# Transposed probabilities copied ahead of the next weight split, and their low part used last in the value product

## The chip, the core and the metric

The kernel runs on one core of one Trainium2 chip. The time is the device time of one launch in microseconds; three timed runs of the kernel before gave 2951.14 us in the median (2946.77 to 2953.13). The changed kernel is timed against it in the same way.

Five engines work side by side, each through its own queue in the order in which the program was written: TensorE (PE, with its weight loads listed apart as PEld), VectorE (DVE), ScalarE (ACT), GpSimd (POOL) and SyncE (SP), which here only issues DMAs. They wait for each other by semaphores.

## What is computed

Two layers of a decoder trunk over 256 tokens of width 2048, all in float32:

```
u = RMSNorm(x);  z = u @ W_in          # parts: cq, ckv+rope key, xb, yb, gate a, gate r
A = causal attention, 16 heads         # low-rank q and kv, a rotary key of 64
R = gelu(yb) * RG-LRU(conv4(xb))
x = x + (sigmoid(ga) * A + sigmoid(gr) * R) @ W_out
x = x + relu(RMSNorm(x) @ W_up)^2 @ W_down
x = x + sigmoid(RMSNorm(x) @ W_pg) * (p[layer] @ W_pe)
```

In the attention, each head has its scores, a softmax `pr`, and the product with the values:

```
pr = softmax(where(causal, sc * scale, -inf))
out = einsum('bhqk,bkhd->bqhd', pr, v)
```

## The kernel before

**Products in three parts.** A float32 operand is split in a high part (rounded to the format that TensorE reads fast) and a low part (the rest). A product is then three matmuls: high weight by high activation, high by low, low by high (`mm3`, L216 to L218).

**Weights in halves.** All weights come in 1004 halves of 128x1024 float32 (512 KB), in the order of use. `half()` hands out the next one. Before it does, it lays out the split of the half that is used two steps later (`split_half`: `hi` on ACT at L122, `lo` on DVE at L126), and then lets the planner (`work`) lay out as many waiting jobs as fit on ACT and DVE within the estimated time of the coming half. There are three buffers each for `hi` and `lo`, so `hi` of half h+2 can only start when TensorE is done with half h-1. A usual half is 24 matmuls.

**Jobs.** `later(key, steps, rank)` puts a job (a row of ACT and DVE steps) in a list by rank; `need(key)` lays out whatever of a job is missing at once (`force`), since TensorE's next instruction depends on it. The planner goes by estimated costs in `E`; what it lays out first stands first in the engine's queue for good.

**The mixer.** Each layer goes through 8 groups of two heads. A group computes xb, yb, k, v, q, the rotary part of q (qr), the recurrence gates (lru), the gates gr and ga, as products from halves; and between the halves of a gate, by hooks, its attention: `scores(0)`, `scores(1)` (tile `s`) in gr, then in ga `turned(0)` after its first half, `values(0)` and `turned(1)` after its second, `values(1)` after its third. In group 0 the late three stand in the xb product of group 1 instead.

`turned(t)` transposes the probabilities of head t on TensorE in three pieces (tile `pt`, L959 to L961) and puts off the job ("pt", t) at rank -2: the copy of the transposed tile to the high part `pt_hi` (ACT, L964), and the rest to `pt_lo` (DVE, L967). `values(t)` needs that job and multiplies (tile `o`): for each of two blocks of keys (256 and 128 query columns) `mm3` with the high and low value tile as weights and `pt_hi`, `pt_lo` as moving data; so the second of its six matmuls reads `pt_lo`. There is one buffer each for `pt_hi`, `pt_lo`, `pt` and `o`.

In group 0, `rot_kr` puts off the rotation of the rotary key (job ("rot", k)), four small ACT copies `sw_k`, three DVE steps, and its split `krk`.

The last group's merged result (`bufB` in layer 0, `bufA` in layer 1, tiles 14 and 15) is read by the product `out` that follows the mixer; its first two pairs of halves go in crossed order, so tiles 14 and 15 are first read at the end of its third half.

Of the kernel before, what the change touches and what calls it, by code (L numbers as in the profile page):

```python
# [18 lines left out]
P = 128  # L19
S = 256  # L20
# [56 lines left out]
def trunk_kernel(ctx: ExitStack, tc: tile.TileContext, xT, pT, pos, par, gfin, invf, wu, out):  # L77
# [13 lines left out]
    V, A, T, G = nc.vector, nc.scalar, nc.tensor, nc.gpsimd  # L91

    def f(ap):
        return ap.bitcast(F32)
# [12 lines left out]
    def load_to(h):  # L107
        while nxt["dma"] <= min(h, n_halves - 1):
            load(nxt["dma"])
            nxt["dma"] += 1  # L110
# [3 lines left out]
    E = {"P": 0.0, "V": 0.0, "A": 0.0, "G": 0.0}  # L114
# [18 lines left out]
    jobs, done = [], {}  # L133
# [3 lines left out]
    class Job:  # L137
# [14 lines left out]
        def step(self, start):  # L152
            eng, cost, fn = self.steps.popleft()
            fn()
            E[eng] = self.ready = start + cost
            if not self.steps:
                jobs.remove(self)
                for k in self.keys:
                    done[k] = self.ready

# [9 lines left out]
    def later(key, *steps, deps=(), rank=1, also=()):  # L170

        job = Job((key, *also), rank, deps, steps)
        at = len(jobs)
        while at and jobs[at - 1].rank > rank:
            at -= 1
        jobs.insert(at, job)

    def need(key):

        if key not in done:  # L180
            next(j for j in jobs if key in j.keys).force()
        E["P"] = max(E["P"], done[key] + LATENCY)
# [19 lines left out]
    def half():  # L202
        h = nxt["used"]
        nxt["used"] += 1
        while nxt["half"] <= min(h + min(LA, max(h - 1, 0)), n_halves - 1):
            split_half(nxt["half"])
            nxt["half"] += 1
        load_to(h + PD)
        work(E["P"] + WINDOW + 0.9, E["P"] + WINDOW)
        hi, lo, at = halves.pop(h)  # L210
        E["P"] = max(E["P"], at)
        return hi, lo

    def mm3(o, wh, wl, ah, al, start, stop, shared=False):

        T.matmul(o, lhsT=wh, rhs=ah, start=start, stop=False, skip_group_check=shared)  # L216
        T.matmul(o, lhsT=wh, rhs=al, start=False, stop=False, skip_group_check=shared)  # L217
        T.matmul(o, lhsT=wl, rhs=ah, start=False, stop=stop, skip_group_check=shared)  # L218
        E["P"] += 0.328
# [371 lines left out]
    def split_steps(d, name, src, tag, cols=512):  # L591


        def high():
            d["src"] = src()
            for w in "hl":
                d[w] = att.tile([P, cols], F32R, name=f"{name}{w}", tag=f"{tag}{w}")
            A.activation(d["h"], d["src"], AF.Copy)

        def low():  # L600
            V.tensor_tensor(out=d["l"], in0=d["src"], in1=f(d["h"]), op=ALU.subtract)

        return ("A", 0.5 if cols > S else 0.3, high), ("V", 0.6 if cols > S else 0.35, low)
# [100 lines left out]
    def group(l, g, u, mg, norm, cn, kr, first, rot_kr):  # L704

        nm = f"{l}_{g}"
        h0 = 2 * g
        t_ = {}
# [93 lines left out]
            rows(ps_k[:, t * S:(t + 1) * S], wt, lambda k: slice(k * 256 + t * P, k * 256 + (t + 1) * P), 1)  # L802
        d_k = t_["k"] = {}
        later(("k", nm), *split_steps(d_k, f"k{nm}", lambda: ps_k, "k"), rank=0)
        hi, lo = half()
        ps_v = mm_bank(f"v_{nm}", ("v", nm))
        for j in range(2):
            o = ps_v[:, j * S:(j + 1) * S]
# [14 lines left out]
            rows(ps_q[:, t * S:(t + 1) * S], wt, lambda k: slice(k * 256 + t * P, k * 256 + (t + 1) * P), 0)  # L823
        d_q = t_["q"] = {}
        later(("q", nm), *split_steps(d_q, f"q{nm}", lambda: ps_q, "q"), rank=0)
        if rot_kr is not None:
            rot_kr()
        wt = half()
        ps_p = bank("r", f"qr_{nm}", ("qr", nm))
        rows(ps_p[:, 0:S], wt, lambda k: slice(k * P, (k + 1) * P), 0)  # L830
# [27 lines left out]
        for t in range(2):  # L858
            ps_l = bank("s", f"lru{t}_{nm}", ("lru", t, nm))
            sl = slice(t * S, (t + 1) * S)  # L860
            for w in range(2):
                c = slice(512 + (2 * w + t) * P, 512 + (2 * w + t + 1) * P)
# [92 lines left out]
        def turned(t):  # L955
            need(("p", t, nm))
            e = t_["p", t]
            pt = bank("t", f"pt{t}_{nm}", ("pt", t, nm))
            T.transpose(pt[:, 256:384], e[:, 256:384], ident)  # L959
            T.transpose(pt[:, 384:512], e[:, 0:128], ident)  # L960
            T.transpose(pt[:, 128:256], e[:, 128:256], ident)  # L961

            def high():
                A.activation(PT[0][:, P:512], pt[:, P:512], AF.Copy)  # L964

            def low():
                V.tensor_tensor(out=PT[1][:, P:512], in0=pt[:, P:512], in1=f(PT[0][:, P:512]), op=ALU.subtract)  # L967

            later(("pt", t, nm), ("A", 0.4, high), ("V", 0.5, low), rank=-2)

        def values(t):
            need(("pt", t, nm))
            need(("v", nm))
            o = bank("o", f"o{t}_{nm}", ("o", t, nm))
            h, lo = PT
            for j, c in ((0, slice(S, 512)), (1, slice(P, S))):
                cc = slice(j * S + t * P, j * S + (t + 1) * P)
                mm3(o[:, j * P:S], t_["v"]["h"][:, cc], t_["v"]["l"][:, cc], h[:, c], lo[:, c], j == 0, j == 1)

            def evac():  # L980
                if t == 0:
                    t_["oT"] = att.tile([P, 512], F32, tag="oT", name=f"oT_{nm}")
                A.activation(t_["oT"][:, t * S:(t + 1) * S], o[:, 0:S], AF.Copy)

            later(("o", t, nm), ("A", 0.27, evac), rank=-1)
# [381 lines left out]
```

## Time and profile before

| what | value |
|---|---|
| median of three runs | 2951.14 us (2946.77 to 2953.13) |
| the profiled execution | 2949.3 us, of it 2947.5 us span from first to last instruction |
| TensorE busy | 2907.9 us, 24800 matmuls |
| VectorE, ScalarE busy | 1864.3 us, 1538.9 us |
| granted TensorE clock | 0.998 of full speed over the span |
| DMA | 535 MB, 182 GB/s in the mean |

TensorE is the engine that the time follows; the other two are busy for 63% and 52% of the span. Matmuls are pipelined: a matmul of 256 columns is shown as 0.28 us long, but the next starts 0.11 to 0.12 us after it. So the idle time that the profile shows in front of a matmul is shorter than what the wait costs: the cost is read from the starts.

### The profile page before, as it was taken

Reading aid. Unit: us, or ns where it says so; the run is one execution under the profiler, and the core shown is the slowest. Engines: PE = TensorE matmul, PEld = TensorE weight load, DVE = VectorE, ACT = ScalarE, POOL = GpSimd, SP = SyncE. Lnnn points to the kernel's source line nnn. Section 1 sums busy time; section 2 is a strip of 40 time slices with the busy share of each in tenths; the row PEclk is TensorE's granted clock in tenths of the full one; section 3 lists DMA queues with packets and bytes.
Section 4 is the critical chain, followed back from the end, with each engine's and each line's share of the span. In section 5 each row is a group of like instructions: output and inputs, shape, how many; then the busy total and the mean of one; then the engine's idle time right before and its main releaser. Section 6 shows DMA issues by size and latency. Waiting matters only on the chain.

```text
span 2947.5 us, 58412 instructions
## 1 busy us (share of the span) xinstructions
PE 2907.9 (99%) x24800; PEld 2896.9 (98%) x24800; DVE 1864.3 (63%) x2420; ACT 1538.9 (52%) x2050; POOL 8.9 (0%) x17
## 2 busy tenths in 40 slices
PE   8999999999999999999999999999999999999998
PEld 8999999999999999999999999999999999999998
DVE  7877777765555454556758777776654555555565
ACT  5666666644344343444546666666543444434445
POOL 0000000000000000000000000000000000000000
PEclk9999999999999999999999999999999999999999
DMA  7555455555555555555555555555555555555553
GB/s 238 168 173 178 165 170 175 172 186 186 186 187 186 186 187 187 191 186 190 190 185 171 173 166 166 174 176 177 189 187 187 186 187 187 188 188 190 186 186 129
DMA packets 146998, 535.23 MB, mean 182 GB/s; under 512 B 16560, under 2 KB 16816, under 8 KB 146736
## 3 DMA queue, kind: packets, MB, share of 16 engines
q1 hardware_dynamic: 146736, 531.50, 54.9%
q8 instruction: 194, 3.18, 0.4%
q14 instruction: 68, 0.56, 0.0%
HBM read 529.33 MB, written 2.10 MB: 180 GB/s over the span
## 4 chain that ended last, share of the span: by engine, by line
PE 93%; DVE 3%; ACT 3%; issue 1%; DMA 0%; ACTq 0%; SPq 0%; POOLq 0%
PE down L218 8%; PE up L218 8%; PE down L217 8%; PE down L216 8%; PE up L216 8%; PE up L217 8%; PE yb L217 2%; PE gr L216 2%; PE yb L218 2%; PE yb L216 2%; PE out L217 2%; PE gr L218 2%; PE out L218 2%; PE gr L217 2%; PE out L216 2%; PE pg L217 2%
## 5 line engine op out<-in xcount | busy, mean ns | idle before, releaser
L126 DVE TENSOR_TENSOR lo<-raw,hi 128x1024 fp32r<-128x1024 f32 x1004 | 1229.8, 1225 | 878.5 <-ACT hi L122 876.3
L122 ACT ACTIVATE hi<-raw 128x1024 fp32r<-128x1024 f32 x1004 | 1066.0, 1062 | 1376.3 <-PE down L217 411.5
L216 PE MATMUL up<-bufA,hi 128*128 128x256 f32 x1024 | 287.9, 281 | 0.0
L216 PE MATMUL down<-bufB,hi 128*128 128x256 f32 x1024 | 287.7, 281 | 0.0
L217 PE MATMUL down<-bufB,hi 128*128 128x256 f32 x1024 | 287.7, 281 | 0.0
L218 PE MATMUL down<-bufB,lo 128*128 128x256 f32 x1024 | 287.7, 281 | 0.0
L216 PE MATMUL down<-bufA,hi 128*128 128x256 f32 x1024 | 287.7, 281 | 0.0
L217 PE MATMUL down<-bufA,hi 128*128 128x256 f32 x1024 | 287.7, 281 | 0.0
L218 PE MATMUL down<-bufA,lo 128*128 128x256 f32 x1024 | 287.7, 281 | 0.0
L216 PE MATMUL up<-bufB,hi 128*128 128x256 f32 x1024 | 287.7, 281 | 0.0
L217 PE MATMUL up<-bufA,hi 128*128 128x256 f32 x1024 | 287.6, 281 | 0.0
L218 PE MATMUL up<-bufA,lo 128*128 128x256 f32 x1024 | 287.6, 281 | 0.0
L218 PE MATMUL up<-bufB,lo 128*128 128x256 f32 x1024 | 287.5, 281 | 0.0
L217 PE MATMUL up<-bufB,hi 128*128 128x256 f32 x1024 | 287.5, 281 | 0.0
L217 PEld LDWEIGHTS down<-bufB,hi 128*128 128x128 f32 x1024 | 196.6, 192 | 0.0
L217 PEld LDWEIGHTS down<-bufA,hi 128*128 128x128 f32 x1024 | 196.6, 192 | 0.0
L217 PEld LDWEIGHTS up<-bufA,hi 128*128 128x128 f32 x1024 | 196.4, 192 | 0.0
L217 PEld LDWEIGHTS up<-bufB,hi 128*128 128x128 f32 x1024 | 196.4, 192 | 0.0
L216 PEld LDWEIGHTS up<-bufA,hi 128*128 128x128 f32 x1024 | 192.3, 188 | 0.0
L218 PEld LDWEIGHTS up<-bufB,lo 128*128 128x128 f32 x1024 | 192.2, 188 | 0.0
L218 PEld LDWEIGHTS up<-bufA,lo 128*128 128x128 f32 x1024 | 192.2, 188 | 0.0
L218 PEld LDWEIGHTS down<-bufB,lo 128*128 128x128 f32 x1024 | 192.2, 188 | 0.0
(551 smaller groups left out, 7857.8 us busy)
## 6 DMA issues: line engine op xcount, KB each, us to landing
raw<-wu SPq DMA_DIRECT2D x1004, 512.0 KB, 3.4
y<-rows SPq DMA_DIRECT2D x4, 512.0 KB, 4.0
x<-xT SPq DMA_DIRECT2D x3, 512.0 KB, 8.2
x<-xT SPq DMA_DIRECT2D x2, 256.0 KB, 4.3
praw<-pT SPq DMA_DIRECT2D x2, 256.0 KB, 4.6
parT<-par SPq DMA_DIRECT2D x1, 184.0 KB, 2.5
rope_w<-pos SPq DMA_DIRECT2D x1, 128.0 KB, 4.1
gf<-gfin SPq DMA_DIRECT2D x1, 8.0 KB, 8.1
```

What stands on the lines that cost most here:

```text
L122: A.activation(hi, src, AF.Copy)
L126: V.tensor_tensor(out=lo, in0=src, in1=f(hi), op=ALU.subtract)
L216: T.matmul(o, lhsT=wh, rhs=ah, start=start, stop=False, skip_group_check=shared)
L217: T.matmul(o, lhsT=wh, rhs=al, start=False, stop=False, skip_group_check=shared)
L218: T.matmul(o, lhsT=wl, rhs=ah, start=False, stop=stop, skip_group_check=shared)
```

## The change

Three things.

1. `turned(t)` no longer puts its copies off. A new helper `at_once` makes the job and lays out its steps right there, so `pt_hi` and `pt_lo` stand in the queues of ACT and DVE ahead of the split that the next `half()` lays out.
2. `values(t)` orders its six matmuls so that the four with `pt_hi` come first and the two with `pt_lo` last; the same six products are summed. The planner's estimate for them is 0.6 instead of 0.656.
3. In group 0, `rot_kr` is called right after k, three halves earlier than before.

```diff
+    def at_once(key, *steps):
+
+        Job((key,), 0, (), steps).force()
@@ turned
-            later(("pt", t, nm), ("A", 0.4, high), ("V", 0.5, low), rank=-2)
+            at_once(("pt", t, nm), ("A", 0.4, high), ("V", 0.5, low))
@@ values
-            for j, c in ((0, slice(S, 512)), (1, slice(P, S))):
-                cc = slice(j * S + t * P, j * S + (t + 1) * P)
-                mm3(o[:, j * P:S], t_["v"]["h"][:, cc], t_["v"]["l"][:, cc], h[:, c], lo[:, c], j == 0, j == 1)
+            vh, vl = (t_["v"][w] for w in "hl")
+            ops = [(v, h, j) for j in range(2) for v in (vh, vl)] + [(vh, lo, j) for j in range(2)]
+            for n, (v, q, j) in enumerate(ops):
+                c = slice(P, S) if j else slice(S, 512)
+                T.matmul(
+                    o[:, j * P:S], lhsT=v[:, j * S + t * P:j * S + (t + 1) * P], rhs=q[:, c], start=n == 0, stop=n == 5,
+                    skip_group_check=True,
+                )
+            E["P"] += 0.6
@@ group
         later(("k", nm), *split_steps(d_k, f"k{nm}", lambda: ps_k, "k"), rank=0)
+        if rot_kr is not None:
+            rot_kr()
...
         later(("q", nm), *split_steps(d_q, f"q{nm}", lambda: ps_q, "q"), rank=0)
-        if rot_kr is not None:
-            rot_kr()
```

What this makes of the queues, at the places of the prediction. First ScalarE's queue in group 6 of layer 0, from the first transposes on (`hi157` and `hi158` are the high parts of two coming weight halves, `zz` and `gr` belong to the recurrence and its gate). Before:

```order
L891 ACTIVATE zz_0_6_6056<-zz_0_6_6056 128x512
L122 ACTIVATE hi157_6157<-raw157_5890 128x1024
L964 ACTIVATE pt_hi_125<-pt0_0_6_6153 128x384
L777 ACT_TABLE_LOAD
L777 ACTIVATE gr_0_6_6126<-gr_0_6_6126 128x512
L122 ACTIVATE hi158_6201<-raw158_5928 128x1024
L964 ACTIVATE pt_hi_125<-pt1_0_6_6197 128x384
```

and the same place on ScalarE now:

```order
L896 ACTIVATE zz_0_6_6056<-zz_0_6_6056 128x512
L969 ACTIVATE pt_hi_125<-pt0_0_6_6153 128x384
L122 ACTIVATE hi157_6159<-raw157_5890 128x1024
L782 ACT_TABLE_LOAD
L782 ACTIVATE gr_0_6_6126<-gr_0_6_6126 128x512
L969 ACTIVATE pt_hi_125<-pt1_0_6_6200 128x384
L122 ACTIVATE hi158_6206<-raw158_5928 128x1024
```

Each of the two `pt_hi` has changed places with the `hi` ahead of it. VectorE's queue at the same place in group 6 (`lo157`, `lo158` are the low parts of those halves, `ee`, `thx` and `hh` belong to the recurrence, L901 is its scan). Before:

```order
L774 TENSOR_TENSOR gr_0_6_6126<-gr_0_6_5923,R_mix0_668 128x512
L126 TENSOR_TENSOR lo157_6158<-raw157_5890,hi157_6157 128x1024
L967 TENSOR_TENSOR pt_lo_126<-pt0_0_6_6153,pt_hi_125 128x384
L894 TENSOR_SCALAR ee_0_6_5935<-ee_0_6_5935 128x512
L895 MEMSET ee_0_6_5935 128x2
L896 SCALAR_TENSOR_TENSOR thx_0_6_5934<-thx_0_6_5934,xc_0_6_5650 128x512
L899 TENSOR_TENSOR thx_0_6_5934<-thx_0_6_5934,zz_0_6_6056 128x512
L901 SCALAR_TENSOR_TENSOR hh_0_6_6208<-ee_0_6_5935,thx_0_6_5934 128x512
L126 TENSOR_TENSOR lo158_6202<-raw158_5928,hi158_6201 128x1024
L967 TENSOR_TENSOR pt_lo_126<-pt1_0_6_6197,pt_hi_125 128x384
```

and VectorE now:

```order
L779 TENSOR_TENSOR gr_0_6_6126<-gr_0_6_5923,R_mix0_668 128x512
L972 TENSOR_TENSOR pt_lo_126<-pt0_0_6_6153,pt_hi_125 128x384
L899 TENSOR_SCALAR ee_0_6_5935<-ee_0_6_5935 128x512
L900 MEMSET ee_0_6_5935 128x2
L901 SCALAR_TENSOR_TENSOR thx_0_6_5934<-thx_0_6_5934,xc_0_6_5650 128x512
L126 TENSOR_TENSOR lo157_6160<-raw157_5890,hi157_6159 128x1024
L972 TENSOR_TENSOR pt_lo_126<-pt1_0_6_6200,pt_hi_125 128x384
L126 TENSOR_TENSOR lo158_6207<-raw158_5928,hi158_6206 128x1024
L904 TENSOR_TENSOR thx_0_6_5934<-thx_0_6_5934,zz_0_6_6056 128x512
L906 SCALAR_TENSOR_TENSOR hh_0_6_6215<-ee_0_6_5935,thx_0_6_5934 128x512
```

The first `pt_lo` now stands ahead of `lo157`, the second ahead of `lo158` and of the scan; the scan is the one that has moved back. Third, VectorE at the end of the last group of layer 0, where the merged tiles 14 and 15 of `bufB` are written, before:

```order
L126 TENSOR_TENSOR lo180_7056<-raw180_6779,hi180_7055 128x1024
L1011 SCALAR_TENSOR_TENSOR bufB_90<-ga_0_7_6972,bufB_90 128x256
L1002 SCALAR_TENSOR_TENSOR ga_0_7_6972<-ga_0_7_6972,oT_0_7_6986 128x256
L1005 SCALAR_TENSOR_TENSOR ga_0_7_6972<-hh_0_7_6978,ga_0_7_6972 128x256
L126 TENSOR_TENSOR lo181_7091<-raw181_6827,hi181_7090 128x1024
L1011 SCALAR_TENSOR_TENSOR bufB_90<-ga_0_7_6972,bufB_90 128x256
L126 TENSOR_TENSOR lo182_7124<-raw182_6879,hi182_7123 128x1024
```

and now:

```order
L1018 SCALAR_TENSOR_TENSOR ga_0_7_6980<-hh_0_7_6985,ga_0_7_6980 128x256
L126 TENSOR_TENSOR lo181_7089<-raw181_6827,hi181_7088 128x1024
L1018 SCALAR_TENSOR_TENSOR ga_0_7_6980<-hh_0_7_6985,ga_0_7_6980 128x256
L126 TENSOR_TENSOR lo182_7120<-raw182_6879,hi182_7119 128x1024
L1024 SCALAR_TENSOR_TENSOR bufB_90<-ga_0_7_6980,bufB_90 128x256 x2
```

The two writes of `bufB`, which stood behind `lo180` and `lo181`, now both stand behind `lo182`; ScalarE's two writes of its high part moved in the same way behind `hi182`. (`hi182` is laid out with half 180, which is the third half of `out`.)

## Rows read from the trace of the kernel before

**Rows 1.** The page: busy time and share of each engine.

```profile
PE 2907.9 (99%) x24800; PEld 2896.9 (98%) x24800; DVE 1864.3 (63%) x2420; ACT 1538.9 (52%) x2050; POOL 8.9 (0%) x17
```

**Rows 2.** Waits of PE and PEld: waiter, releaser, us in total, times, longest.

```profile
PE o L217 <- DVE pt_lo L967: 15.4, 28, 1.0
PE s L926 <- DVE qs L847: 2.3, 2, 1.2
PE pt L959 <- DVE p L951: 1.7, 2, 0.9
...
PEld o L217 <- DVE pt_lo L967: 21.5, 30, 1.2
```

**Rows 3.** Timeline, PE, group 6: start, length, instruction [idle before <- releaser].

```profile
484.68 0.27 PE L961 MATMUL pt<-ident,p 128*128 128x128 f32 x1
...
487.53 0.28 PE L216 MATMUL o<-pt_hi,v_6h 128*128 128x256 f32 x1
488.25 0.39 PE L217 MATMUL o<-pt_lo,v_6h 128*128 128x256 f32 x1 [0.45 <-DVE pt_lo L967]
488.48 0.28 PE L218 MATMUL o<-pt_hi,v_6l 128*128 128x256 f32 x1
```

**Rows 4.** Timeline, PE: `values(1)` in groups 4 to 7 of layer 0.

```profile
369.68 0.39 PE L217 MATMUL o<-pt_lo,v_4h 128*128 128x256 f32 x1 [0.54 <-DVE pt_lo L967]
...
430.98 0.39 PE L217 MATMUL o<-pt_lo,v_5h 128*128 128x256 f32 x1 [0.55 <-DVE pt_lo L967]
...
491.98 0.28 PE L216 MATMUL o<-pt_hi,v_6h 128*128 128x256 f32 x1
492.88 0.39 PE L217 MATMUL o<-pt_lo,v_6h 128*128 128x256 f32 x1 [0.63 <-DVE pt_lo L967]
...
555.12 0.39 PE L217 MATMUL o<-pt_lo,v_7h 128*128 128x256 f32 x1 [0.97 <-DVE pt_lo L967]
```

**Rows 5.** Timeline, ACT, group 6.

```profile
485.43 1.05 ACT L122 ACTIVATE hi<-raw 128x1024 fp32r<-128x1024 f32 x1
486.38 0.47 ACT L964 ACTIVATE pt_hi<-pt 128x384 fp32r<-128x384 f32 x1
...
488.70 1.04 ACT L122 ACTIVATE hi<-raw 128x1024 fp32r<-128x1024 f32 x1
```

**Rows 6.** Timeline, DVE, group 6.

```profile
486.51 1.23 DVE L126 TENSOR_TENSOR lo<-raw,hi 128x1024 fp32r<-128x1024 f32 x1 [0.90 <-ACT hi L122]
487.65 0.55 DVE L967 TENSOR_TENSOR pt_lo<-pt,pt_hi 128x384 fp32r<-128x384 f32 x1
...
489.30 0.69 DVE L899 TENSOR_TENSOR thx<-thx,zz 128x512 f32<-128x512 f32 x1
490.02 1.22 DVE L901 TENSOR_TENSOR_SCAN hh<-ee,thx 128x512 f32<-128x512 f32 x1
491.16 1.20 DVE L126 TENSOR_TENSOR lo<-raw,hi 128x1024 fp32r<-128x1024 f32 x1
492.28 0.55 DVE L967 TENSOR_TENSOR pt_lo<-pt,pt_hi 128x384 fp32r<-128x384 f32 x1
```

**Rows 7.** Windows in `out`, layer 0, then 1: busy us (count) per engine, PEclk, DMA.

```profile
560.00:660.00 100.00, 100.00 (x851) 100.00 (x850) 61.94 (x73) 48.45 (x62) 0.00 (x0) 1.00 0.56 187
2019.00:2119.00 100.00, 100.00 (x885) 100.00 (x884) 63.96 (x76) 50.07 (x64) 0.00 (x0) 1.00 0.57 192
```

**Rows 8.** Timeline of ACT, then DVE, in the second half of `out`, layer 0.

```profile
561.58 1.06 ACT L122 ACTIVATE hi<-raw 128x1024 fp32r<-128x1024 f32 x1 [1.20 <-issue]
...
562.67 1.23 DVE L126 TENSOR_TENSOR lo<-raw,hi 128x1024 fp32r<-128x1024 f32 x1 [0.52 <-ACT hi L122]
563.82 0.42 DVE L1011 SCALAR_TENSOR_TENSOR bufB<-ga,bufB 128x256 fp32r<-128x256 f32 x1
```

**Rows 9.** Timeline, PE: the second and the third half of `out` begin, layer 0.

```profile
561.45 0.28 PE L216 MATMUL out<-bufB,hi 128*128 128x256 f32 x1
...
564.28 0.28 PE L216 MATMUL out<-bufB,hi 128*128 128x256 f32 x1
```

More of the change, by code (lines that the diff above doesn't have):

```diff
@@ L156, in step @@
             if not self.steps:
-                jobs.remove(self)
+                if self in jobs:
+                    jobs.remove(self)
                 for k in self.keys:
```

## Prediction

> **What bounds the kernel now.** I read the page first, then the waits of TensorE, then the three queues around the dearest of these waits. The page says where time can be won at all: TensorE is busy for 2907.9 of 2947.5 us, VectorE and ScalarE for 63% and 52% [rows 1]. So an edit pays only where it shortens an idle stretch of TensorE, or makes its matmuls follow each other more closely.
>
> The waits of TensorE are led by one: the second matmul of `values` waits for `pt_lo`, 28 times, 15.4 us; its weight load, which waits for the same thing, 30 times, 21.5 us [rows 2]. There are 32 such places (16 groups, two heads), so it is nearly all of them. Idle time understates it. In group 6 the first matmul of `values(0)` starts at 487.53, the second at 488.25, the third at 488.48 [rows 3]; unhindered they would follow at some 0.115. So the stop costs 0.605 and the restart another 0.115, together 0.72, where the row shows 0.45 idle: 0.27 more than the idle. In `values(1)` the step from 491.98 to 492.88 gives 0.79, with the restart 0.90, where 0.63 is shown [rows 4].
>
> Why `pt_lo` is late is read from the two other queues. The transposes are done at 484.95 [rows 3]. ScalarE is free for the next thing at 485.43, and that is a weight half (`hi`, 1.05); `pt_hi` comes at 486.38 [rows 5]. VectorE then does `lo` of that half, 486.51 with 1.23, and only then `pt_lo`, 487.65 to 488.20 [rows 6]: 0.6 after TensorE has come to it. For the second head the queue is longer: `thx`, the scan (1.22) and another `lo` stand ahead of `pt_lo`, 492.28 to 492.83 [rows 6].
>
> **The copies ahead of the split (and `pt_lo` last).** I put the new order on the times of group 6. `pt_hi` takes the slot at 485.43 and ends at 485.90; `pt_lo` follows at about 485.93 and ends at 486.48 (0.55). `values(0)` starts at 487.53 and now reads `pt_lo` only at its fifth matmul, some 0.4 later: over 1.0 us to spare, nothing waits. Before, three matmuls and three transposes followed the one at 488.48, at 0.11 each and 0.27 for the last one's length: done at 489.41. TensorE is now 0.72 ahead, so 488.69. ScalarE is free at 488.70, where `hi` started [rows 5]: `pt_hi` to 489.17, `pt_lo` to about 489.75. `values(1)` would start at 491.98 - 0.72 = 491.26: 1.5 us to spare. Both waits go, each with a cover of its own even if the new order of the six matmuls were not there; that order alone would be worth some 0.4 of each wait. Its own cost: the same six matmuls and loads in another mix of 256 and 128 columns, at most one step of 0.05 either way each, 32 x 0.05 = 1.6 us either way; I take 0, since the row of loads sets the pace in both.
>
> The sum over the kernel: 15.4 idle plus 28 x 0.27 = 23.0, and the two places where only the load shows a wait (30 against 28), 0.3 each: 23.6 us. The 28 agree with each other: 0.45 at `values(0)`, 0.54 to 0.63 at `values(1)`, 0.97 in the last group [rows 3, 4]. Bounds: 21.5, the idle time of the loads [rows 2], and 24. **Term: -23.6.**
>
> What pays for it: each passed `hi` starts 0.4 later and its `lo`, now behind `pt_lo` and the steps up to 489.30 less 487.65 = 1.65 after it, ends near 485.93 + 1.65 + 1.23 = 488.81 instead of 487.74. That half is used after `values(1)`, near 491.9: 3.1 us of cover. `lo` of the next half ends near 491.4, used near 494.7. The raw buffers come back one microsecond later; six of them stand between SP's queue and the split, some 16 us, so the DMA does not notice. The scan starts 2 us later (492.0 for 490.02). Its result meets only the merge, which TensorE first reads in `out`; that is free in groups 0 to 6.
>
> **The end of the last group.** There it isn't free. Both `bufB` writes now stand behind the split of half 182, whose `hi` cannot start before the third half of `out` does. On the row of the half before it, `hi` starts 0.13 after its half (561.58 to 561.45), `lo` 1.09 after that, `bufB` 1.15 after that, for 0.42 [rows 8, 9]: 0.13 + 1.09 + 1.15 + 0.42 = 2.79 after the start of the third half. TensorE wants the low part of tile 14 after six tiles and one matmul: a half is 564.28 - 561.45 = 2.83 [rows 9], so 6/8 x 2.83 + 0.12 = 2.24. A new stop of 0.55, with restart some 0.65; tile 15 is written 0.33 later and read 0.35 later. Two layers: **+1.3**, between 0 (if `hi` gets its buffer earlier) and 2.6 (twice that).
>
> **The rotation of the key in group 0.** It takes four ACT copies and a split out of the way of q's rotation, on which scores wait (2.3 us, twice [rows 2]): so that wait should shrink, between not at all and to nothing. Against it: in that group the exponentials of head 1 stand behind the swapped pair `pt_hi` and `hi` on ScalarE, and `pt_hi` has to wait for its transposes first; as `hi` slips by 0.4 in group 6, the wait for `p` (1.7, twice) should grow by up to 0.4 per layer. I take half of the 2.3 as gone and 0.8 as added. **Term: -0.4**, bounds -2.3 and +0.8.
>
> **The pace.** Matmuls of 256 columns run at two paces, with the clock granted in full in both. The window in `out` of layer 0 holds 851 of them in 100 us, the one in layer 1 885 [rows 7]: 117.5 and 113.0 ns each, same code, no wait in either. A pace lasts until something breaks the stream, and after the stops in `values(1)` it came out either way. It shows in the distance of one group to the next: 430.98 - 369.68 = 61.30 where the fast pace followed, 492.88 - 430.98 = 61.90 where the slow one did [rows 4]. By such distances nine of the fourteen groups-to-next are slow and five fast. With the stops gone, every group meets the same stream, so I expect one pace for most. All fast would give 9 x 0.6 = 5.4, and 4.5 ns x some 850 matmuls = 3.8 in `out` of layer 0: -9. All slow would cost 5 x 0.6 = 3.0 and 3.8 in `out` of layer 1: +7. Nothing in the trace says which; I take 0 and keep both ends.
>
> The Trainium skill (TensorE: Matmul & The Clock Gate, Back-to-back issue gap) gives one isolated spacing for 256 columns at the full clock, N/2.4 + 2.5, estimated 109 ns. By it there is one pace and this term is zero on both sides; the 113.0 and 117.5 of the two windows speak against that.
>
> **Sum.** 2949.3 of the profiled execution: -23.6 + 1.3 - 0.4 = -22.7, so 2926.6. The median of the runs, 2951.14, lies 1.8 above the profiled execution: 2928.4, taken as 2928. A time within 0.2% (5.9 us, about what a measurement of this kernel can tell from no change) would be 2945.2 to 2957.0.
>
> **Rivals.**
> - *The fast pace follows everywhere.* For it: five of fourteen, and nothing stops the stream in `values` any more. 2928 - 9 = 2919.
> - *The slow pace follows everywhere.* For it: nine of fourteen. 2928 + 7 = 2935.
> - *The copies are still late.* The order shows them ahead, but the second `pt_hi` stands behind a table load and `gr`'s tanh on ScalarE; it would have to slip by the 1.5 us of cover before TensorE waits. If every `values(1)` kept its wait (about 13 of the 23.6) the time is 2928 + 13 = 2941.
> - *Slower: the split is late.* ScalarE's queue now holds a copy that waits for TensorE in front of the weights that TensorE needs two halves on. It decides from where the split comes 3.1 us later than I put it. For a time over 2957 it must cost over 29 us; 32 are 1.07 us at each of 30 places, a split 4.2 us late, while the order puts 0.47 of ScalarE and 1.65 of VectorE in front. The Trainium skill (same page, section on the 16 sub-arrays) calls these two queues strict first in, first out, which is how this would come about; the row where `pt_hi` waits behind `hi` agrees [rows 5]. It gives 2960.
>
> **How the numbers follow.** Forecast 0.42 (2924 to 2932); fast pace 0.27; slow pace 0.22; still late 0.06; slower 0.03. The range runs from the fast pace with the lower bounds of the small terms, 2919 - 4, to the slow pace with their upper ones, 2935 + 3: 2915 to 2938. Left out are most of the last two cases and the tails, under 2 in 10. Faster by over 0.2% is all but the slower case and a part of the late one: 0.94; same 0.04; slower 0.02.
>
> **What would show it.** Right: the line of `o` waiting for `pt_lo` is gone or under 2 us; `pt_hi` starts within 1 us of the last transpose; a wait of `out` for `bufB` of about 0.5 us appears in each layer; the wait for `qs` shrinks and that for `p` grows. The two windows in `out` tell the pace: 851 or 885. Wrong: a new line of TensorE waiting for `lo` (L126), or for `oT` through the one buffer of `o`, of more than 2 us.

## The result, and the profile after

| | before | after |
|---|---|---|
| median of the runs | 2950.16 us (4 runs, 2946.77 to 2953.13) | 2925.02 us (4 runs, 2923.96 to 2925.61) |
| ratio, 95% interval | | 0.9915 (0.9898 to 0.9932) |
| profiled execution, span | 2949.3, 2947.5 us | 2925.61, 2923.8 us |

The change makes the kernel 0.85% faster, 25 us; forecast were 2928 us, in a range of 2915 to 2938. The page of after answers to [rows 1]: TensorE's busy time falls by 9.4 us, the rest of the 23.7 us of span was idle time.

```profile
PE 2898.5 (99%) x24800; PEld 2893.3 (99%) x24800; DVE 1860.8 (64%) x2420; ACT 1536.2 (53%) x2050; POOL 8.9 (0%) x17
```

The waits of PE after (waiter, releaser, us in total, times, longest), to be held against [rows 2]:

```profile
PE pt L964 <- DVE p L956: 2.6, 2, 1.3
...
PE s L931 <- DVE qs L852: 1.2, 2, 0.6
...
PE out L222 <- DVE bufA L1024: 0.5, 1, 0.5
...
PE out L222 <- DVE bufB L1024: 0.4, 1, 0.4
```

The line of `o` waiting for `pt_lo` is gone altogether. The wait for `qs` has halved (2.3 to 1.2), that for `p` has grown (1.7 to 2.6), and a wait of `out` for the merged tiles has come in, once per layer.

The same place as [rows 3, 5, 6], group 6 of layer 0, some 7 us earlier now. PE:

```profile
477.41 0.27 PE L966 MATMUL pt<-ident,p 128*128 128x128 f32 x1
...
480.26 0.28 PE L987 MATMUL o<-pt_hi,v_6h 128*128 128x256 f32 x1
...
480.67 0.39 PE L987 MATMUL o<-pt_lo,v_6h 128*128 128x256 f32 x2
...
483.98 0.28 PE L987 MATMUL o<-pt_hi,v_6h 128*128 128x256 f32 x1
...
484.62 0.33 PE L221 MATMUL ga<-bufA,hi 128*128 128x256 f32 x1
```

ACT, where `pt_hi` now stands ahead of `hi`, and the evacuation of `o` (`oT`) behind both:

```profile
478.16 0.47 ACT L969 ACTIVATE pt_hi<-pt 128x384 fp32r<-128x384 f32 x1
...
481.44 0.49 ACT L969 ACTIVATE pt_hi<-pt 128x384 fp32r<-128x384 f32 x1
481.83 1.05 ACT L122 ACTIVATE hi<-raw 128x1024 fp32r<-128x1024 f32 x1
482.77 0.38 ACT L996 ACTIVATE oT<-o 128x256 f32<-128x256 f32 x1
```

DVE:

```profile
478.66 0.56 DVE L972 TENSOR_TENSOR pt_lo<-pt,pt_hi 128x384 fp32r<-128x384 f32 x1 [0.33 <-ACT pt_hi L969]
...
480.20 1.22 DVE L126 TENSOR_TENSOR lo<-raw,hi 128x1024 fp32r<-128x1024 f32 x1
481.96 0.56 DVE L972 TENSOR_TENSOR pt_lo<-pt,pt_hi 128x384 fp32r<-128x384 f32 x1 [0.55 <-ACT pt_hi L969]
482.91 1.23 DVE L126 TENSOR_TENSOR lo<-raw,hi 128x1024 fp32r<-128x1024 f32 x1 [0.39 <-ACT hi L122]
```

`pt_lo` ends at 479.22 for a `values(0)` that starts at 480.26 (1.04 to spare, forecast "over 1.0") and at 482.52 for a `values(1)` at 483.98 (1.46, forecast 1.5); `pt_hi` starts 0.48 behind the last transpose (477.41 + 0.27). The `lo` that was passed ends at 481.42, 3.2 ahead of the half of `ga` that reads it, at 484.62 (forecast 3.1). One number was not in the forecast: `oT`, which frees the single `o`, ends at 483.15, only 0.83 ahead of that `values(1)`.

The new stop in `out`, layer 0: first PE, then DVE:

```profile
555.55 0.28 PE L221 MATMUL out<-bufB,hi 128*128 128x256 f32 x1
556.27 0.39 PE L222 MATMUL out<-bufB,hi 128*128 128x256 f32 x1 [0.44 <-DVE bufB L1024]
```

```profile
554.66 1.22 DVE L126 TENSOR_TENSOR lo<-raw,hi 128x1024 fp32r<-128x1024 f32 x1 [1.27 <-ACT hi L122]
555.80 0.75 DVE L1024 SCALAR_TENSOR_TENSOR bufB<-ga,bufB 128x256 fp32r<-128x256 f32 x2
```

It lies where it was put, behind the split's `lo`. The windows in `out` (span, then busy us and count for PE, PEld, DVE, ACT, POOL, then PEclk, DMA share, GB/s), layers 0 and 1, answer to [rows 7]: 881 in 100 us and 752 in 85 us, so 113.5 and 113.0 ns each, both at the fast pace. (`out` has 768 matmuls a layer, so windows of this length run on into `up`, here and in [rows 7].)

```profile
560.00:660.00 100.00, 100.00 (x881) 99.95 (x880) 62.61 (x75) 50.24 (x63) 0.70 (x1) 1.00 0.58 193
2005.00:2090.00 85.00, 85.00 (x752) 85.00 (x751) 54.55 (x65) 44.16 (x56) 0.00 (x0) 1.00 0.58 192
```

**The account.** Over both traces I took each step from one matmul's start to the next one's that is longer than 0.16 us, less the usual 0.1125, and summed by place. For `values`, whose steps are of several lengths, I took the whole time from the start of the first of its six matmuls to the start of what follows them, over 30 places (at the other two the wait for `p` follows): 42.5 us before, 19.2 after, and 19.1 in the run below that has the early copies with the old order (e2). So the waits cost 23.4, and the new order by itself 0.1. The account of the span:

| term | forecast | measured |
|---|---|---|
| waits for `pt_lo` | -23.6 | -23.4 |
| stop in `out`, both layers | +1.3 | +1.5 (0.71 and 0.80) |
| group 0: q / p | -1.2 / +0.8 | -1.1 / +0.85 |
| steps of the new order | 0 | +0.1 |
| pace and rest (what is left) | 0 | -1.6 |
| span | -22.7 | -23.7 |
| from the profiled execution to the median | +1.8 | -0.6 |

Below, "slow" and "fast" matmuls are counted from the starts in the same way: six in a row with a mean step over 116 ns, or under, and none over 135 ns. Where the sixes begin shifts such a count by some per cent.

### The profile page after: what moved, and what is told of

It is laid out like the page before. It is cut to its first block, busy times and chain, and to the rows that moved or that the text cites. A ratio compares the mean times of both kernels' runs of the same rounds, so it can differ in the third digit from the quotient of the medians.

```text
span 2923.8 us, 58376 instructions
## 1 busy us (share of the span) xinstructions
PE 2898.5 (99%) x24800; PEld 2893.3 (99%) x24800; DVE 1860.8 (64%) x2420; ACT 1536.2 (53%) x2050; POOL 8.9 (0%) x17
## 5 line engine op out<-in xcount | busy, mean ns | idle before, releaser
L222 PEld LDWEIGHTS down<-bufB,hi 128*128 128x128 f32 x1024 | 196.6, 192 | 0.0
L222 PEld LDWEIGHTS up<-bufB,hi 128*128 128x128 f32 x1024 | 196.4, 192 | 0.0
L221 PEld LDWEIGHTS up<-bufB,hi 128*128 128x128 f32 x1024 | 192.2, 188 | 0.0
L221 PEld LDWEIGHTS down<-bufB,hi 128*128 128x128 f32 x1024 | 192.2, 188 | 0.0
```

## The experiments

The kernel before was run again on each chip: 2953.04 us for `e1` to `e4`, 2945.85 for `e5` to `e8`, 2953.84 for `e10` to `e13` (single runs 2939.59 to 2956.11). Most of the changed kernels repeat within 2 us, e3, e5 and e6 within 5 to 8. The changed kernel itself (after) was not timed again beside them, so differences of a few us between runs of different chips are read from the traces, and the medians only agree or disagree with them.

### The parts one by one

**e1_low_last: the kernel before, with the new order of the six matmuls alone.**

```diff
-            for j, c in ((0, slice(S, 512)), (1, slice(P, S))):
...
-                mm3(o[:, j * P:S], ... h[:, c], lo[:, c], j == 0, j == 1)
...
+            ops = [(v, h, j) for j in range(2) for v in (vh, vl)] + [(vh, lo, j) for j in range(2)]
...
```

> The kernel before with only the new order of the six matmuls in values (low part last); the copies are still put off. My theory (the place of the copies in the queues is the cause): TensorE reads pt_lo four matmuls into values instead of one, about 0.28 us later, so each of the 30 waits shrinks by 0.28 and none goes: about -8 us, 2942; the line of o waiting for pt_lo still shows some 28 waits. Rival (the order of the matmuls is what brings the gain): 2925 to 2928 and no wait left.

Measured: 2942.11 us (2941.89 to 2943.7), ratio 0.9965 (0.9952 to 0.9978). Its waits of PE:

```profile
PE o L980 <- DVE pt_lo L967: 9.2, 20, 0.7
```

So the order alone takes 6.2 of the 15.4 us and leaves 20 stops (some 28 were expected). By the starts the 30 places fall from 42.5 to 34.6 us: 7.8 of the 23.4, or 0.26 for each place, near the 0.28 that was expected of it and not the 0.4 of the prediction, which counted from the first matmul, where the wait had stood at the second.

**e2_at_once: the kernel before, with the copies laid out early alone** (old order of the six, rotation at its old place).

```diff
+    def at_once(key, *steps):
...
-            later(("pt", t, nm), ("A", 0.4, high), ("V", 0.5, low), rank=-2)
+            at_once(("pt", t, nm), ("A", 0.4, high), ("V", 0.5, low))
```

> The kernel before with only the copies laid out at the transposes; old order of the six matmuls, rotation of the key where it was. My theory: all 30 waits for pt_lo go, since there was 1.0 to 1.5 us to spare without the new order; 2925 to 2929, the wait of scores for qs back at 2.3, that of out for the merged tile smaller than in the changed kernel (one of the two writes stands ahead of the third half's split). Rival (the order of the matmuls matters as much): 2935 or more, with waits for pt_lo at values(1) left.

Measured: 2918.55 us (2917.84 to 2918.9), ratio 0.9884 (0.9868 to 0.9901): 6.5 us less than the whole change, and as much below the range expected of it. Its waits of PE:

```profile
PE pt L964 <- DVE p L956: 2.6, 2, 1.3
PE s L931 <- DVE qs L852: 2.3, 2, 1.1
...
PE out L222 <- DVE bufA L1016: 0.2, 1, 0.2
```

No wait of `o`: each wait does have its cover without the new order, as forecast. The longer wait for `p` (2.6) comes from the copies; the one for `qs` is untouched without the rotation. And it beats the whole change, which none of the cases had: its span is 6.9 us shorter (2916.9 to 2923.8). The six matmuls of `values(1)` in group 6, with the first that follows, take as long in the old order (482.36 to 482.99) as in the new one (483.98 to 484.62 after, shown above):

```profile
482.36 0.28 PE L221 MATMUL o<-pt_hi,v_6h 128*128 128x256 f32 x1
...
482.99 0.33 PE L221 MATMUL ga<-bufA,hi 128*128 128x256 f32 x1
```

Where the time goes, a window in `xb` of group 7 shows. After:

```profile
488.00:496.00 8.00, 8.00 (x71) 8.00 (x70) 6.27 (x8) 3.80 (x5) 0.00 (x0) 1.00 0.58 198
```

and e2:

```profile
488.00:496.00 8.00, 8.00 (x73) 8.00 (x73) 5.87 (x8) 3.71 (x4) 0.00 (x0) 1.00 0.56 188
```

71 against 73 in 8 us. Of the 3072 matmuls of `xb` and `yb`, 2196 are slow in after and 240 in e2; in the gates `gr` it is the other way round, 438 and 1200. In the spans the slower `xb` and `yb` cost the whole change 8.6 us; `gr` and `ga` give 2.9 back, the rotation 1.1; the longer stop in `out` costs 0.9; 1.4 lie elsewhere.

What the order of the six does to the pace is seen at the ends of 14 groups a trace, from the last 24 matmuls ahead of `values(1)` to the 24 behind it. With the old order and no wait (e2, and e6, e7, e13 below) they are fast on both sides, 56 times of 56. With the new order and no wait (after, and e3, e4, e10, e12 below) the pace turns round at all 70 places: 52 times from fast to slow, 18 times from slow to fast. So the new order leaves the slow pace where the fast one stood ahead of it, which is most places.

**e11_rot_only: the kernel before, with the rotation of the key early alone.**

```diff
         later(("k", nm), *split_steps(d_k, f"k{nm}", lambda: ps_k, "k"), rank=0)
+        if rot_kr is not None:
+            rot_kr()
...
         later(("q", nm), *split_steps(d_q, f"q{nm}", lambda: ps_q, "q"), rank=0)
-        if rot_kr is not None:
-            rot_kr()
```

> The kernel before with the rotation of the key in group 0 called right after k alone. Theory: the wait for qs falls from 2.3 us to about 1.2 in two places, the wait for p stays at 1.7, the 28 waits for pt_lo stay at 15.4; about 1 us of 2950, too little for the timer (2945 to 2953). Rival (the copies laid out at once, not the rotation, shorten q's wait): qs stays at 2.3. A second rival, that the rotation and not the copies makes p later: p rises to 2.6.

Measured: 2947.49 us (one run), too near for the timer; the trace decides:

```profile
PE o L217 <- DVE pt_lo L967: 15.1, 28, 1.0
...
PE pt L959 <- DVE p L951: 1.8, 2, 0.9
...
PE s L926 <- DVE qs L847: 1.2, 2, 0.6
```

`qs` halves by the rotation alone, and `p` stays. With e2 this splits the group 0 term: -1.1 for the rotation, +0.85 for the copies.

### What sets the pace

**e3_merge_ahead: after, without the new stop in `out`:** the last two merges are laid out ahead of the split of its third half.

```diff
+        def ahead():
+            for k in (14, 15):
+                for j in list(jobs):
+                    if (act[1], k) in j.keys and name.startswith("out"):
+                        j.force()
...
-                ps = mm_pair(f"{name}_{pr}", keys[0], act, (), pr == 0)
+                ps = mm_pair(f"{name}_{pr}", keys[0], act, (None, ahead) if pr == 0 else (), pr == 0)
```

> The changed kernel, with the last two merges laid out ahead of the split of out's third half (both writes of the last two merged tiles stand ahead of that split). My theory: the wait of out for the merged tiles (0.5 and 0.4 idle, 1.5 us with the restarts) goes. If nothing else moves: 2923.5. But the break in the stream is what put out in the fast pace in layer 0: without the break out may run slow there (117.5 ns, 851 matmuls in 100 us), which costs 3.7 us a layer: up to 2931. Rival (out's pace is not decided by breaks): 2923.5 with out as fast as before in both layers.

Measured: 2927.11 us (2924.3 to 2931.39), ratio 0.9915 (0.99 to 0.993): not faster for a wait less. No wait of `out` is left in the profile, but its two windows in `out` are slow (75 us / 639 = 117.4 ns):

```profile
560.00:635.00 75.00, 75.00 (x639) 75.00 (x638) 46.68 (x55) 37.90 (x48) 0.00 (x0) 1.00 0.57 186
2010.00:2085.00 75.00, 75.00 (x640) 75.00 (x639) 46.30 (x54) 37.90 (x48) 0.00 (x0) 1.00 0.55 185
```

In after, layer 0, the 66 matmuls of `out` ahead of the stop at 556.27 step by 117.8 ns, the 699 behind it by 113.4: there the stop of 0.7 us was followed by the fast pace, 3.1 us, worth more than it cost. In layer 1 `out` ran fast ahead of its stop already (113.3), so e3's slow pace there came with the group before it and not from the missing stop. Nor does such a stop always end in the fast pace: of the 18 in nine traces (two layers each; after, e2, and e4 to e6, e8, e10, e12, e13 below) 15 have it behind them, three the slow one, as in layer 0 of e6, fast ahead of its stop (113.3 ns) and behind it at 65 us / 554 = 117.3 ns:

```profile
565.00:630.00 65.00, 65.00 (x554) 65.00 (x553) 41.04 (x48) 32.27 (x42) 0.00 (x0) 1.00 0.56 187
```

The profiled run of e3 is the slowest of the four; the others lie up to 7 us lower, and their pace wasn't seen.

**e4_tick_spread: after, with two matmuls of one column behind each spread of a norm's factor** (`rb`). Their weights are a part of the mask that holds zeros, so they add nothing to their accumulator.

```diff
+            if kk == 3 and nxt.pop("tick", None):
+                for _ in range(2):
+                    T.matmul(o[:, 0:1], lhsT=mask[:, 0:P], rhs=ones[:, 0:1], start=False, stop=False, skip_group_check=True)
...
+            nxt["tick"] = True
```

> The changed kernel, with two matmuls of one column (zero weights, so they add nothing) put in the stream 12 matmuls after each spread of a norm's factor. In the traces the pace was slow after each of these spreads, through the whole of up and down (12288 matmuls in both layers), and fast after the one-column matmuls of a norm's root. Theory 1 (the pace is a state that a break in the stream sets and that lasts): fast pace in up and down, 4.5 ns x 12288 = -55 us, 2870. Theory 2 (the pace belongs to the stage, its data or the traffic beside it): 2925 to 2926, up and down at 281 ns and 117.8 apart as before. A fall back to the slow pace after some of the chunks would give something between.

Measured: 2872.41 us (2871.43 to 2873.4), ratio 0.9728 (0.9714 to 0.9743). Two tiny matmuls at each of eight places (four spreads a layer; the expectation of e13 says six) take 52.6 us off. The windows in `up`, 350 us behind such a place; after, then e4:

```profile
1000.00:1080.00 80.00, 80.00 (x681) 80.00 (x681) 43.56 (x43) 37.08 (x43) 0.00 (x0) 1.00 0.57 186
```

```profile
1000.00:1080.00 80.00, 80.00 (x708) 80.00 (x707) 45.24 (x44) 38.52 (x44) 0.00 (x0) 1.00 0.59 195
```

80 us / 681 = 117.5 ns and 80 / 708 = 113.0, at a clock of 1.00 in both. The place itself, in e4's queue of PE:

```profile
655.57 0.59 PE L554 MATMUL rb_mlp<-dg_mlp,ones 128*128 128x256 f32 x2
...
656.12 0.28 PE L222 MATMUL up<-bufA,hi 128*128 128x256 f32 x1
...
657.29 0.28 PE L223 MATMUL up<-bufA,lo 128*128 128x256 f32 x1
657.41 0.50 PE L237 MATMUL up<-ones,mask 128*128 128x1 f32 x4
657.77 0.36 PE L221 MATMUL up<-bufA,hi 128*128 128x256 f32 x1
```

Between `rb` and the short matmuls ten steps take 656.12 to 657.29, 117 ns each; behind them the fast pace holds to the end of `down`, but for 12 matmuls. The pair is shown as four instructions and puts 657.77 - 657.29 = 0.48 us between two matmuls, 0.37 more than usual. In after, 11946 of the 12288 matmuls of `up` and `down` are slow, in e4 12: 11934 x 4.5 ns = 53.7 us, less 8 x 0.37 = 2.9 for the pairs; some matmuls elsewhere turned too, and 52.6 were measured. In every trace here the first matmuls behind each of the eight spreads are slow and those ahead of it fast. So in `up` and `down` the pace is a state of the stream: something sets it, and it stays until something else does. That this holds everywhere is not shown: k, v and q, below, are slow whatever comes ahead.

**e5_tick_values: after, with the same two matmuls behind each `values(1)`.**

```diff
+            if kk == 3 and nxt.pop("tick", None):
+                tick(o)
...
+            if t == 1:
+                nxt["tick"] = True
```

> The changed kernel, with two one-column matmuls (zero weights) 12 matmuls after each values(1), nowhere else. The kernel with the copies early but the old order of the six matmuls ran 6.5 us faster than the changed kernel, and its trace shows xb and yb of nearly every group in the fast pace, where the changed kernel shows them slow in 11 of 14 groups. Theory 1 (the new order costs time by the pace that it leaves behind): the two matmuls bring the fast pace back after values; 11 x 0.6 = -6.6 plus 16 x 0.15 for the matmuls themselves, 2920 to 2921. Theory 2 (the new order is dearer in itself, the pace is chance): 2925 to 2928.

Measured: 2928.07 us (2925.45 to 2933.67), ratio 0.9946 (0.9928 to 0.9964) to a kernel before that ran at 2945.85: no gain. The first half came true, `xb` has turned fast (e5, to be held against after's 71):

```profile
488.00:496.00 8.00, 8.00 (x73) 8.00 (x72) 6.02 (x9) 4.04 (x5) 0.00 (x0) 1.00 0.45 158
```

but the gain of 7.8 us in `xb` and `yb` went elsewhere. The pairs cost 0.37 us each, as in e4, and not the 0.15 that was put for them: 16 x 0.37 = 5.9. `gr` lost 3.4 (slow are 1200 of its 1536 matmuls here, 438 in after), and `out`, slow in one layer, 2.8. Together that is 4.3 us more than after, where the spans differ by 4.7. So the time, though it is that of theory 2, doesn't decide between them. The traces do: the new order is not dearer in itself (the six take the same time, above), and behind all 16 pairs the matmuls are fast, at 12 of them slow ahead of it. Between `yb` and `gr` stand k, v and q, which step by some 117 ns in every kernel here (but for 48 matmuls of e7); the kernels that enter them slow mostly leave them fast (after, e4), and the other way round (e2, e5). Why was not found.

### Where the cover ends

**e8_act_later: after, with five ACT copies of 128x128 behind each `pt_hi`** (1.67 us, ahead of the split's `hi`), to find how much room the splits have.

```diff
+            def held():
+                high()
+                for _ in range(5):
+                    A.activation(scratch, mask[:, 0:P], AF.Copy)
-            at_once(("pt", t, nm), ("A", 0.4, high), ("V", 0.5, low))
+            at_once(("pt", t, nm), ("A", 0.4, held), ("V", 0.5, low))
```

> The changed kernel, with five small ACT copies (128x128, into a scratch tile that nobody reads) behind each pt_hi, so that the weight split behind it and all that follows on ScalarE starts later, by 0.8 to 1.5 us a time (no row shows such a copy; a 128x256 copy took 0.37). My theory: 3.1 us of cover at the split and 1.5 us at the second pt_lo take it; no wait for lo of a split, time 2925 to 2930 (the pace may move). Rival (the split is near its edge): waits for lo or hi, 0.8 us or more at 30 places, 2950.

Measured: 2972.59 us (one run), 47 us over after. Neither the theory (no wait) nor the rival (a split late) held. Waits of PE:

```profile
PE o L993 <- ACT oT L1002: 30.4, 15, 2.2
...
PE pt L965 <- DVE p L957: 5.8, 2, 2.9
```

ACT in group 6, then the first matmul of `values(1)`:

```profile
501.18 0.47 ACT L970 ACTIVATE pt_hi<-pt 128x384 fp32r<-128x384 f32 x1
501.55 1.67 ACT L979 ACTIVATE scratch<-mask 128x128 f32<-128x128 f32 x5
503.12 1.04 ACT L122 ACTIVATE hi<-raw 128x1024 fp32r<-128x1024 f32 x1
504.06 0.36 ACT L1002 ACTIVATE oT<-o 128x256 f32<-128x256 f32 x1
```

```profile
504.48 0.39 PE L993 MATMUL o<-pt_hi,v_6h 128*128 128x256 f32 x1 [2.17 <-ACT oT L1002]
```

There is one buffer for `o`, and the copy that frees it stands behind the late `hi`. Not the split but this evacuation is next to the edge: 0.83 us in after.

The waits shown are not all of the 47 us: by the starts the 15 stops cost 34.5, the wait for `p` 3.2 more than in after. And behind seven of the stops in `o` and the one for `p`, of 2.2 to 3.1 us each from start to start, the granted clock reads 0.50 (1.2 and not 2.4 GHz). Behind the stop at 504.48:

```profile
505.50:508.50 3.00, 3.00 (x16) 3.00 (x16) 2.96 (x4) 0.30 (x1) 0.00 (x0) 0.50 0.54 179
```

Some 16 matmuls follow each other there at 213 ns in place of 113: 1.6 us a time, 13 us for the eight. (34.5, 3.2 and 13 are more than 47; elsewhere this run's pace is some 3 us better.)

**e10_oT_ahead: the same copies, with `oT` of head 0 laid out ahead of them.**

```diff
                 high()
+                if t == 1:
+                    need(("o", 0, nm))
```

> The kernel of the run with five ACT copies behind each pt_hi, with one difference: the evacuation of the first head's o (oT) is laid out ahead of those copies, not behind them and the split. Theory (the evacuation through the single buffer of o is what stood too close): the line of o waiting for oT, 30.4 us over 15 places, falls under 2 us, no line of TensorE waiting for hi or lo of over 2 us appears, and the time comes down from 2972.6 to 2925 to 2935 (the wait for p, 5.8, may stay). Rival (the splits themselves are late by the copies): a new line of PE waiting for hi or lo of over 10 us, time over 2940.

Measured: 2943.59 us (one run). 29 us of the 47 go with one copy moved; the line of `oT` is gone, and with it seven of the eight stretches at half the clock, so the buffer was the cause. But a line has taken its place that the theory had excluded, as the rival said, though under its 10 us:

```profile
PE xb L223 <- DVE lo L126: 7.0, 12, 0.6
```

```profile
498.38 0.39 PE L223 MATMUL xb<-bufA,lo 128*128 128x256 f32 x1 [0.58 <-DVE lo L126]
```

```profile
495.24 1.22 DVE L907 TENSOR_TENSOR_SCAN hh<-ee,thx 128x512 f32<-128x512 f32 x1
...
497.11 1.22 DVE L126 TENSOR_TENSOR lo<-raw,hi 128x1024 fp32r<-128x1024 f32 x1
```

With 2 x 1.68 + 0.38 = 3.7 us more of ACT in the way the splits are 0.6 us late, and not those beside the copies but the next one, whose `lo` stands behind the scan (495.24) and one more step of the recurrence. That fits a room of some 3 us (3.7 - 0.6), near the 3.1 that the prediction gave; since DVE's order has changed too, it is not known to a tenth. The time was missed by 9 us (2925 to 2935 expected): these waits, 7.0 us shown, cost 10.3 by the starts.

### Put together

**e6_combined: copies early, old order of the six, rotation early, short matmuls as in e4** (the difference to after is shown).

```diff
+            nxt["tick"] = True
...
-            ops = [(v, h, j) for j in range(2) for v in (vh, vl)] + [(vh, lo, j) for j in range(2)]
...
+            for j, c in ((0, slice(S, 512)), (1, slice(P, S))):
...
+                mm3(o[:, j * P:S], ... h[:, c], lo[:, c], j == 0, j == 1)
```

> Copies early, old order of the six matmuls, rotation of the key early, and the two one-column matmuls after each spread. If the gains add (6.5 of the old order, less the rotation's 1.1 that was missing there, 52.6 of the one-column matmuls): 2872.4 - 6.5 - 1.1 = 2864.8. If the old order's gain is chance of the pace: up to 2872.

Measured: 2866.5 us (2864.03 to 2868.78), ratio 0.9734 (0.9719 to 0.9749), as expected.

**e7_combined_k: e6 with the merges ahead as in e3, a short pair in each k and one in `c` of layer 0** (the difference to e6 is shown).

```diff
+            if l == 0 and n == 1:
+                nxt["tick"] = True
...
+                if k == 1 and nxt.pop("tick_rows", None):
+                    tick(o)
...
+        nxt["tick_rows"] = True
...
-                ps = mm_pair(f"{name}_{pr}", keys[0], act, (), pr == 0)
+                ps = mm_pair(f"{name}_{pr}", keys[0], act, (None, ahead) if pr == 0 else (), pr == 0)
```

> The combined kernel, with two more one-column matmuls in each k product (and once near the start), and the last two merges ahead of the split of out's third half. In every trace so far k, v and q (1152 matmuls) and mostly gr after them ran slow, from the first half of k on, whatever came before. Theory 1 (the pace is a state that a break sets): k, v, q, the rest of that half and gr turn fast; 4.5 ns x (1536 + up to 1200) = -12 us, plus 0.15 x 16 = +2.4, and -0.9 for the wait in out: about 2854. Theory 2 (something in k itself keeps it slow): no gain there, 2866 with the added matmuls.

Measured: 2866.66 us (2866.17 to 2867.73), ratio 0.9736 (0.9719 to 0.9752): nothing won where 12 us were expected. `gr` (42 slow of 1536) and `out` (none) did turn fast, 4146 slow matmuls went down to 2052, but k, v and q stayed slow but for 48: of the two theories the second holds for them. The added pairs cost 0.37 us a place and not 0.15. By the traces `gr`, `ga` and `out` are 9.2 us shorter and k is 7.5 longer, 16 x 0.37 = 5.9 of it the pairs. The traced spans differ by 2.3 (2867.0 and 2864.7); e6's is the slowest of its four runs, so that the medians show nothing of it.

**e12_combined_low_last: e6 with the new order of the six back in** (the difference to e6 is shown).

```diff
-            for j, c in ((0, slice(S, 512)), (1, slice(P, S))):
...
-                mm3(o[:, j * P:S], ... h[:, c], lo[:, c], j == 0, j == 1)
...
+            ops = [(v, h, j) for j in range(2) for v in (vh, vl)] + [(vh, lo, j) for j in range(2)]
...
```

> The combination (copies early, old order of the six matmuls, rotation early, one-column matmuls after each spread of a norm's factor; 0.9734 of the kernel before) with the new order of the six matmuls put back. Theory 1 (the new order costs only its own steps, 32 places of some 0.06 us): 1.8 us more, 2868, ratio about 0.974. Theory 2 (the new order also leaves the slow pace behind in the gates gr and ga and the next group's xb and yb): some 6.5 us more, 2873, ratio about 0.9756, with xb and yb mostly slow.

Measured: 2872.9 us (2872.55 to 2874.18), the 2873 of theory 2 and 6.4 above e6 (4.2 by the traced spans). The ratios, 0.9726 (0.9711 to 0.974) and e6's 0.9734, don't show it, since the kernel before ran 8 us apart on the two chips; e13 ran beside e12, has the old order and lies 10.1 below, of which its fewer short matmuls are 1.8 (8 x 0.22), so that the order is worth some 8 there. The window in `xb` tells why, e12:

```profile
488.00:496.00 8.00, 8.00 (x70) 8.00 (x70) 6.27 (x8) 4.23 (x5) 0.00 (x0) 1.00 0.61 197
```

1584 of `xb` and `yb` are slow, in e6 18. The time of the six is the same here too (19.2 and 19.1 us over the 30 places), so theory 1 had no 1.8 us to add. Only half of `xb` and `yb` is slow: at 7 of the 14 places `values(1)` turned the slow pace into the fast one. That the new order costs time by the pace is thus seen twice, with the short matmuls in `up` and without.

**e13_one_tick: e6 with one short matmul at each of the eight places instead of two** (the difference to e6 is shown).

```diff
     def tick(o):
-        for _ in range(2):
+        for _ in range(1):
```

> The combination with one one-column matmul at each of its six places instead of two. Theory (one short matmul is enough to bring the fast pace): up and down all fast, time as with two, 2866, ratio 0.973. Rival (two in a row are needed): up and down stay at the slow pace, some 52 us more, 2918, ratio 0.989.

Measured: 2862.85 us (2862.55 to 2863.04), ratio 0.9691 (0.9675 to 0.9707), the fastest kernel of this study, 62 us below the changed one. One is enough (`up` and `down`: 12 slow). It is 3.7 us below e6, its traced span 6.3: 918 slow matmuls fewer (`out` is fast in both layers here, in one there) give 4.1, and eight shorter breaks, 0.26 us from start to start in place of 0.48, give 1.8.

## Why the prediction was right, and where its steps were not

**The waits.** -23.6 forecast, -23.4 measured. The step that carried it was to read the cost from the starts: the idle time shown was 15.4, the places lost 23.4. That the copies alone remove all of them, with 1.0 and 1.5 us to spare, e2 and the rows of group 6 bear out. That the order alone is worth 0.4 of each was too much (0.26).

**The stop in `out`.** +1.3 forecast, +1.5 measured, at the matmul and for the reason given. What was missed is its second effect: in layer 0 the fast pace followed the break, and without the break it stayed away (e3).

**Group 0.** Both halves came out as put, q by -1.1, p by +0.85, and e11 and e2 give each its cause.

**The new order of the six.** Its own steps were taken as nothing, "at most one step of 0.05 either way each [...] I take 0", and that came out: 0.1 us over the 30 places. The reason given, that the row of loads sets the pace in both, no run tests. What the sum had no term for is what the order does to the pace behind it: at `values(1)` the new order turned it round each time, mostly to the slow one. That makes most of the 6.5 us between e2 and after, and of the 8 by which e12 lies above e13 for its order. With the copies early, the new order has nothing left to cover: in these runs the change would have been better without its second part.

**The pace.** Taken as 0, with -9 and +7; what the trace gives is about -1.9, and that it lies near 0 is luck: two effects, one from each end of its range, partly cancel. 699 matmuls of `out` in layer 0 turned fast behind the new stop (-3.1), and 11 instead of 9 of the 14 group-to-next distances are slow (2 x 0.6 = +1.2). The prediction's 3.8 for `out` counted the "some 850" matmuls of a 100 us window; `out` has 768 a layer, which gives 3.5. That a pace lasts until something breaks the stream came out in `up` and `down`, not in k, v and q. "One pace for most" held; which, the trace of before couldn't say. Left aside was the larger thing: [rows 7] were read as a term of plus or minus 9 in the groups and `out`, while `up` and `down`, half of all matmuls, sat at the slow pace before and after alike. For this change that is no error, but it was the largest gain in this study.

**The rivals.** *Still late*: no wait of `o` is left. *Split late*: no line of `lo` in after, where its cover is 3.2 us; e10 fits that. But the place nearest the edge, `oT` with 0.83 us, stood only in the list of what would show the forecast wrong, with no number. *Fast* and *slow everywhere*: half of each, `out` fast, groups slow; e2, with the fast pace in `xb`, `yb` and `out`, comes to 2918.6 where *fast* gave 2919.

**The last 3 us** between 2928.4 and 2925.0: the span came 1.0 shorter than forecast (pace and rest -1.6, the other terms +0.6 together), and the median lay 0.6 below the profiled execution where 1.8 above was taken over from before.

## What to carry to other kernels

Where an engine waits for a copy that only stands behind other work in its queue, lay the copy out first; then ask again whether a second remedy for the same wait is still needed, since it may cost what it no longer saves. Before moving work ahead in a queue, list every later instruction in it that frees a single buffer, since that one, not the big transfer, may have the least cover. And divide the length of a few stall-free windows by their matmuls: two values for the same code show time that no list of waits names. Where two orders of the same matmuls are compared, take the whole time from the first to what follows: the new order has one step of 0.17 us at each place that the old one hasn't, and gives it back in the others.

## What the runs showed of the hardware

The same stream of 256-column matmuls, with no wait and a granted clock of 1.00, runs at 113.0 or 117.5 ns each, and keeps to one for hundreds of microseconds. Here the spread of a norm's factor (`rb`) left the slow one at all eight places of every trace; one matmul of a single column (two instructions in the profile, 0.14 us more between its neighbours) the fast one (e13: 12 slow of 12288 in `up` and `down`); a stop for data in `out` the fast one at 15 of 18 places; the new order of `values(1)`, with no wait in it, the other one than stood ahead of it (70 of 70). k, v and q stayed at some 117 ns in all runs but for 48 matmuls of e7, short matmuls in the middle of k or not. The cause below this isn't shown. The Trainium skill (TensorE: Matmul & The Clock Gate, Back-to-back issue gap) gives measured spacings of such streams of loads and matmuls, 81 ns for 128 columns and 131 for 512; the two windows, at 256 columns, lie between them.
